# Merge gates and branch projections of a hybrid decoder layer: weights as the moving operand, 1024 columns a unit

## The chip, the cores and the metric

The kernel runs on one core of one Trainium2 chip. The metric is the device time of one execution in microseconds (us). A core has TensorE (matrix multiply; it has a queue for matmuls, PE, and one for loading the stationary operand, PEld), VectorE (DVE), ScalarE (ACT), GpSimd (POOL) and SyncE (SP). In this kernel SP issues nearly all loads and POOL the stores of intermediate results. TensorE writes into PSUM, which the kernel uses as eight banks of 128 partitions x 512 float32: four for the large sums (pool `acc`) and four for small work (pool `mx`).

## What is computed

One decoder layer on 256 tokens with a model width of 4096, in float32. The reference, cut to what matters here (`hgrn2_mix` and `diff_attention` are the two token mixers):

```
u = rmsnorm(h, norm_w[l])                       # [256, 4096]
proj = u @ w_in[l]                              # 10 parts: a_q a_f a_i a_g b_q b_k b_v b_g gate_a gate_b
o_a = hgrn2_mix(a_q, a_f, a_i, lb_all[l])
o_a = rmsnorm(o_a, hgrn_norm_w[l]) * silu(a_g)          # [256, 2048]
o_b = diff_attention(qb, kb, vb, lam, slopes)
o_b = rmsnorm(o_b, subln_w[l]) * (1 - lam_init) * silu(b_g)   # [256, 2048]
y = (sigmoid(gate_a) * (o_a @ w_branch_a[l])    # gate_a, gate_b: [256, 4096]
     + sigmoid(gate_b) * (o_b @ w_branch_b[l]))
h = h + y @ w_out[l]
return rmsnorm(h, final_w)
```

The change touches the projections to `gate_a` and `gate_b` (4096 rows of weights and 4096 columns each) and the two branch projections (2048 rows and 4096 columns each).

## The kernel before

**The stream of weights.** All weights pass through the core once, in pieces of 128 partitions x 2048 float32 (1 MB), 512 pieces in all. SP loads a piece into one of three raw buffers (tile `w`, line 105), up to three pieces ahead. Each piece is split in two halves of 1024 columns. For each half ScalarE writes a rounded part `hi` (line 123) and VectorE the rest, `lo = w - hi` (line 124), both in a format that TensorE takes in one pass. There are four buffers of `hi` and four of `lo`, and the splits run three halves ahead. The activations are split in the same way: `u` (and later `oh` for the outputs of the mixers, `y` for the merged rows) holds for each 128 channels a high and a low part of 256 tokens. A product is then three products: high x hi, high x lo and low x hi.

**Two forms of unit.** In a *stationary* unit (`stat_unit`, `branch_unit`, and `kout_unit` for the forget gates) a 128x128 block of `hi` is loaded into TensorE and the 512 columns of the activations, high and low parts together, move past it (line 184); then the block of `lo` is loaded and the 256 columns of the high part move (line 185). The result has channels as partitions and tokens as columns, in two halves of one bank that must be added (`sum_halves`: ScalarE copies one half, VectorE adds). In a *moving* unit (`mov_unit` with `mov_mm`) 128 tokens of the activations are stationary and 512 columns of weights move, three matmuls for each token block (lines 255 to 257). The result has tokens as partitions.

**The stages.** First come four groups of branch A and four of branch B, with the mixers' small work in between. Then come the merge gates, 64 stationary units of two pieces each; two of them make a tile `gt`, which is scaled, put through a sigmoid and stored to DRAM by POOL (line 286). During this stage the mixers' outputs are reloaded and split into `oh`. Then follow the branch projections, 32 stationary units of two pieces: each loads its gates (tile `gl`, lines 653 and 654), multiplies, adds the two branches and splits the sum into `y`, which has the layout that the output projection wants. The output projection is made of moving units.

**What sets the order.** The program walks through the list of pieces (`run`); for each it issues loads and splits ahead, then the matmuls of both halves, then one step of background work from a list (`todo`). A scheduler then gives each engine its order, which the engine keeps; the splits have a higher priority.

Of the kernel before, what the change touches and what calls it, by code (L numbers as in the profile page):

```python
# [44 lines left out]
def trunk_kernel(ctx, tc, xT, x, nw, w_stat, w_mov, w_a, w_b, w_out, lbt, hnw, lamv, slw, fw, out):  # L45
# [8 lines left out]
    ev = ctx.enter_context(tc.tile_pool(name="ev", bufs=3))  # L54
    gp = ctx.enter_context(tc.tile_pool(name="gp", bufs=2))
# [4 lines left out]
    def f32(ap):  # L60
        return ap.bitcast(F32)

# [124 lines left out]
    def sum_halves(ps, dst=None):  # L187
        t = ev.tile([P, S], F32, name="half", tag="half")
        act.activation(t, ps[:, S:], AF.Copy)
        dst = t if dst is None else dst  # L190
        dve.tensor_tensor(dst, ps[:, :S], t, op=ALU.add)
        return dst
# [82 lines left out]

    def gate_unit(q):
        T = {}

        def gate_done(j):
            def d(ps):  # L280
                if j == 0:
                    T["g"] = gp.tile([P, 2, S], F32, name="gt", tag="gt")
                scaled(ps, T["g"][:, j])
                act.activation(T["g"][:, j], T["g"][:, j], AF.Sigmoid)
                if j == 1:
                    pool.dma_start(g_dram[q], T["g"])
            return d

        for j in range(2):
            stat_unit(48 + q * 2 + j, gate_done(j))  # L290

# [8 lines left out]
    g_dram = [dram.tile([P, 2, S], F32, name=f"g_dram{g}") for g in range(32)]  # L300
# [28 lines left out]
    # ======================= projections and mixers =========================  # L329
    with tc.tile_pool(name="tmp", bufs=1) as tmp:  # L330
# [14 lines left out]
        def finish(T, seg, eps, scale, slot):  # L345
            """rms norm over segments of the channels, times silu of the gate; transposed and out to DRAM."""
# [37 lines left out]
        def rows_done(T, k, then):  # L384
            """Scaled rows out of a unit with the weights moving."""
# [8 lines left out]
        # The 64-token chunks go in pairs. Within a pair the decays count from its middle: exp(b - b_last) and  # L394
        # exp(b_last - b) in the even chunk, exp(b) and exp(-b) in the odd one. From the first pair to the second
        # the keys are decayed to the end of theirs, the queries from the start of theirs.
# [223 lines left out]
        for q in range(4):  # L620
            gate_unit(q)
# [4 lines left out]
    with tc.tile_pool(name="op", bufs=1) as op:  # L626
        oh = [op.tile([P, 4, 2, S], F32R, name=f"oh{g}") for g in range(8)]

        def o_load(g):
            t = op.tile([P, 4, S], F32, name="ol", tag="ol", bufs=2)  # L630
            nc.sync.dma_start(t, o_dram[g])
            return t

        def o_split(g, t):
            act.activation(oh[g][:, :, 0, :], t, AF.Copy)
            dve.tensor_tensor(oh[g][:, :, 1, :], t, f32(oh[g][:, :, 0, :]), op=ALU.subtract)

        ol = {}
        for g in range(8):
            todo.extend([lambda g=g: ol.update({g: o_load(g)}), None, None, lambda g=g: o_split(g, ol.pop(g))])  # L640
        for q in range(4, 32):
            gate_unit(q)

# [1 line left out]
        y = []  # L645

        def branch_unit(m):
            st = {}

            def fn(n, hi, lo):  # L650
                if n == 0:
                    gt = op.tile([P, 2, S], F32, name="gl", tag="gl", bufs=2)
                    nc.sync.dma_start(gt[:, 0], g_dram[m // 2][:, m % 2])
                    nc.sync.dma_start(gt[:, 1], g_dram[16 + m // 2][:, m % 2])
                    st["g"] = gt
                    if m % 4 == 0:
                        y.append(uy.tile([P, 4, 2, S], F32R, name="y", tag="uy"))
                if n % 2 == 0:
                    st["ps"] = acc.tile([P, 512], F32, name="ps_b", tag="acc")
                ps = st["ps"]  # L660
                for k in range(8):
                    kt = 8 * n + k
                    mm_stat(ps, hi[:, k * P : (k + 1) * P], lo[:, k * P : (k + 1) * P], oh[kt // 4], kt % 4,
                            kt % 16 == 0, kt % 16 == 15)
                if n % 2 == 0:
                    return
# [153 lines left out]
```

## Time and profile before

| what | value |
|---|---|
| median of three runs | 2903.52 us (2902.39 to 2905.15) |
| span of the profiled execution (the page gives no other time of it) | 2923.0 us |
| TensorE busy, matmuls | 2909.9 us, 15254 |
| VectorE, ScalarE, GpSimd busy | 1561.8, 1361.9, 97.4 us |
| gate stage, first and last matmul | 1474.63 to 2201.6 us |
| branch stage, first and last matmul | 2201.7 to 2563.4 us |
| output projection, first and last matmul | 2563.5 to 2911.8 us |
| moved by DMA | 583.38 MB, 200 GB/s on average |

In a group of instructions the fields are: line, engine, operation, output tile <- input tiles, shapes, count | busy time in us, mean duration in ns | idle time of the engine just before these instructions, and what ended it. A row of the timeline has start, duration, engine and instruction, and in brackets the idle time before it and what ended it. A row of the stretches has the stretch and its length, then the busy time and count for PE, PEld, DVE, ACT and POOL, the granted clock of TensorE, the busy share of the DMA engines and GB/s. A row of the DMA issues ends with the KB of each and the median us from issue to landing.

### The profile page before, as it was taken

The numbers are of one execution on the slowest core, as the hardware profiler recorded it, in microseconds if no ns is written. First come the engines' busy times: TensorE is split into PE (matmuls) and PEld (weight loads), VectorE is DVE, ScalarE is ACT, GpSimd is POOL, SyncE is SP. The second block draws the span as 40 slices with busy tenths as digits, with TensorE's granted clock in tenths as the row PEclk, the third lists the DMA queues.
The fourth block names the chain that finished last, engine by engine and source line by source line (L and its number), as shares of the span: only waits on it lengthen the run. The fifth ranks groups of instructions, "written<-read, shape, count | busy, mean of one in ns | idle before, by whom it ended". The sixth has DMA issues, their size and how long they took to land.

```text
span 2923.0 us, 37440 instructions
## 1 busy us (share of the span) xinstructions
PE 2909.9 (100%) x15254; PEld 2483.7 (85%) x15254; DVE 1561.8 (53%) x1745; ACT 1361.9 (47%) x1675; POOL 97.4 (3%) x113
## 2 busy tenths in 40 slices
PE   9999999999999999999999999999999999999998
PEld 8888888888888888888888888888888888888886
DVE  6545455464555555555556454545546666654454
ACT  7545454454444444444454444444444444444443
POOL 0000000000000000000000000000000000001010
PEclk9999999999999999999999999999999999999999
DMA  8555555555555555555566555555556556566654
GB/s 333 186 187 187 185 189 180 182 193 187 182 185 185 193 181 190 181 183 194 185 212 241 196 196 200 201 198 198 202 198 207 211 206 211 207 226 210 211 209 173
DMA packets 95277, 583.38 MB, mean 200 GB/s; under 512 B 11376, under 2 KB 19840, under 8 KB 30080
## 3 DMA queue, kind: packets, MB, share of 16 engines
q1 hardware_dynamic: 89568, 562.10, 55.2%
q0 software_dynamic: 5536, 18.89, 1.7%
q8 instruction: 119, 1.95, 0.3%
q14 instruction: 54, 0.44, 0.0%
HBM read 564.17 MB, written 16.78 MB: 199 GB/s over the span
## 4 chain that ended last, share of the span: by engine, by line
PE 95%; issue 3%; DMA 1%; ACT 0%; DVE 0%; POOL 0%; SPq 0%; DVEq 0%; POOLq 0%; ACTq 0%
PE ps_s L184 27%; PE ps_s L185 14%; PE ps_m L255 11%; PE ps_m L256 11%; PE ps_m L257 11%; PE ps_b L184 8%; PE ps_b L185 4%; PE ps_k L184 4%; PE ps_k L185 2%; DMA ol<-o_dram 1%; PE ps_sc L454 0%; PE ps_s L543 0%; PE ps_o L469 0%; DMA o_dram<-oT 0%; PE ps_t L373 0%
## 5 line engine op out<-in xcount | busy, mean ns | idle before, releaser
L124 DVE TENSOR_TENSOR lo<-w,hi 128x1024 fp32r<-128x1024 f32 (+1 forms) x1026 | 1266.7, 1236 | 1292.5 <-ACT hi L123 1291.7
L123 ACT ACTIVATE hi<-w 128x1024 fp32r<-128x1024 f32 (+1 forms) x1026 | 1082.8, 1056 | 1479.4 <-PE ps_s L184 636.9
L184 PE MATMUL ps_s<-u,hi 128*128 128x512 f32 x3584 | 1264.2, 398 | 0.0
L185 PE MATMUL ps_s<-u,lo 128*128 128x256 f32 x3584 | 1007.3, 281 | 0.4 <-DVE lo L124 0.4
L184 PEld LDWEIGHTS ps_s<-u,hi 128*128 128x128 f32 x3584 | 672.9, 188 | 163.5
L185 PEld LDWEIGHTS ps_s<-u,lo 128*128 128x128 f32 x3584 | 677.0, 189 | 1.1 <-DVE lo L124 0.8
L255 PE MATMUL ps_m<-hi,u 128*128 128x512 f32 x1024 | 402.1, 393 | 0.0
L256 PE MATMUL ps_m<-lo,u 128*128 128x512 f32 x1024 | 398.7, 389 | 0.0
L257 PE MATMUL ps_m<-hi,u 128*128 128x512 f32 x1024 | 398.7, 389 | 0.0
L184 PE MATMUL ps_b<-oh,hi 128*128 128x512 f32 x1024 | 361.9, 399 | 0.0
L185 PE MATMUL ps_b<-oh,lo 128*128 128x256 f32 x1024 | 287.6, 281 | 0.0
L184 PEld LDWEIGHTS ps_b<-oh,hi 128*128 128x128 f32 x1024 | 192.4, 188 | 47.9
L257 PEld LDWEIGHTS ps_m<-hi,u 128*128 128x128 f32 x1024 | 192.2, 188 | 40.5
L255 PEld LDWEIGHTS ps_m<-hi,u 128*128 128x128 f32 x1024 | 192.3, 188 | 39.5
L256 PEld LDWEIGHTS ps_m<-lo,u 128*128 128x128 f32 x1024 | 192.3, 188 | 39.0
L255 PE MATMUL ps_m<-hi,y 128*128 128x512 f32 x504 | 196.1, 389 | 0.0
L256 PE MATMUL ps_m<-lo,y 128*128 128x512 f32 x504 | 196.1, 389 | 0.0
L257 PE MATMUL ps_m<-hi,y 128*128 128x512 f32 x504 | 196.1, 389 | 0.0
L185 PEld LDWEIGHTS ps_b<-oh,lo 128*128 128x128 f32 x1024 | 193.4, 189 | 0.0
L184 PE MATMUL ps_k<-u,hi 128*128 128x512 f32 x512 | 180.9, 400 | 0.5 <-DVE u L146 0.4
L185 PE MATMUL ps_k<-u,lo 128*128 128x256 f32 x512 | 141.2, 282 | 0.0
L184 PEld LDWEIGHTS ps_k<-u,hi 128*128 128x128 f32 x512 | 95.8, 188 | 23.9 <-ACT hi L123 1.9
(174 smaller groups left out, 1283.6 us busy)
## 6 DMA issues: line engine op xcount, KB each, us to landing
w<-in_w_stat SPq DMA_DIRECT2D x224, 1024.0 KB, 4.9
w<-in_w_mov SPq DMA_DIRECT2D x156, 1024.0 KB, 4.9
w<-in_w_out SPq DMA_DIRECT2D x64, 1024.0 KB, 4.9
w<-in_w_a SPq DMA_DIRECT2D x32, 1024.0 KB, 5.0
w<-in_w_b SPq DMA_DIRECT2D x32, 1024.0 KB, 4.9
g_dram<-gt POOLq DMA_DIRECT2D x32, 256.0 KB, 3.7
gl<-g_dram SPq DMA_DIRECT2D x64, 128.0 KB, 4.5
o_dram<-oT POOLq DMA_DIRECT2D x8, 512.0 KB, 6.9
```

Of the source, the lines that this page charges most:

```text
L123: act.activation(hi[:, c : c + m], t[:, c : c + m], AF.Copy)
L124: dve.tensor_tensor(lo[:, c : c + m], t[:, c : c + m], f32(hi[:, c : c + m]), op=ALU.subtract)
L184: pe.matmul(ps, wh, ut[:, k].rearrange("p a s -> p (a s)"), start=first, stop=False)
L185: pe.matmul(ps[:, :S], wl, ut[:, k, 0, :], start=False, stop=last)
L255: pe.matmul(ps[t], uh, wh, start=first, stop=False)
L256: pe.matmul(ps[t], uh, wl, start=False, stop=False)
L257: pe.matmul(ps[t], ul, wh, start=False, stop=last)
```

## The change

Gates and branch projections become `wide_unit`s: moving units with 1024 columns of weights. A half piece now holds 128 rows of weights and 1024 columns, as two column halves. For each column half and each of two token blocks there are three matmuls of 512 columns, so that a unit fills all four `acc` banks. The matmuls of a unit's last two half pieces are issued together, bank by bank, and each bank is read out as soon as its six are issued. There are 8 gate units of 16 pieces and 8 branch halves of 8 pieces (for each of four column ranges one of branch A, then one of branch B); the pieces are as many and as large as before.

A gate is now one sigmoid on ScalarE straight from PSUM, which scales by a value for each token, and a store for each 128 x 512 block. At the end of a branch A half VectorE multiplies the four banks by their gates; at the end of a B half it multiplies and adds. As the rows now have tokens as partitions and the output projection needs channels there, each merged 128 x 512 block is turned by four transposes on TensorE (`turn`), a background step, and split into `y` from PSUM. The mixers' outputs are reloaded in 16 blocks of 256 KB in place of 8 of 512 KB, into the four buffers that the gates use too; gates are loaded in four blocks of 256 KB for each branch half.

```diff
-    ev = ctx.enter_context(tc.tile_pool(name="ev", bufs=3))
-    gp = ctx.enter_context(tc.tile_pool(name="gp", bufs=2))
+    gp = ctx.enter_context(tc.tile_pool(name="gp", bufs=4))
...
     def sum_halves(ps, dst=None):
-        t = ev.tile([P, S], F32, name="half", tag="half")
+        t = gp.tile([P, S], F32, name="half", tag="gt")
...
+    def wide_unit(srcs, src_tiles, done):
+        st = {}
+        last = 2 * len(srcs) - 1
+
+        def cols(r, n):
+            c = n if r % 2 else 1 - n
+            return slice(c * 512, (c + 1) * 512)
+
+        def fn(r, hi, lo):
+            if r == 0:
+                st["ps"] = [[acc.tile([P, 512], F32, name="ps_w", tag="acc") for _ in range(2)] for _ in range(2)]
+            ps = st["ps"]
+            if r < last - 1:
+                for n in range(2):
+                    c = cols(r, n)
+                    mov_mm([ps[t][n] for t in range(2)], src_tiles[r // 4], r % 4, hi[:, c], lo[:, c], r == 0, False)
+                return
+            st[r] = hi, lo
+            if r < last:
+                return
+            for n in range(2):
+                for t in range(2):
+                    for k in (last - 1, last):
+                        hi, lo = st[k]
+                        c = cols(k, n)
+                        mov_mm({t: ps[t][n]}, src_tiles[k // 4], k % 4, hi[:, c], lo[:, c], False, k == last, (t,))
+                    done(t, n, ps[t][n])
+
+        add(srcs, fn)
+
     def gate_unit(q):
...
-        for j in range(2):
-            stat_unit(48 + q * 2 + j, gate_done(j))
...
+        def done(t, n, ps):
+            g = gp.tile([P, 512], F32, name="gt", tag="gt")
+            act.activation(g, ps, AF.Sigmoid, scale=rstd[:, t : t + 1])
+            pool.dma_start(g_dram[2 * q + n][t], g)
+
+        wide_unit([w_gate[q, n] for n in range(16)], u, done)
...
-        def branch_unit(m):
...
+        def branch_unit(q):
+            rows, g = {}, {}
+
+            def g_load(br):
+                for n in range(2):
+                    for t in range(2):
+                        gl = g[t, n] = op.tile([P, 512], F32, name="gl", tag="gl", bufs=4)
+                        nc.sync.dma_start(gl, g_dram[8 * br + 2 * q + n][t])
+
+            def a_done(t, n, ps):
+                r = rows[t, n] = gp.tile([P, 512], F32, name="yr", tag="gt")
+                dve.tensor_tensor(r, ps, g[t, n], op=ALU.mult)
+
+            def b_done(t, n, ps):
+                r, gl = rows[t, n], g[t, n]
+                dve.tensor_tensor(gl, ps, gl, op=ALU.mult)
+                dve.tensor_tensor(r, r, gl, op=ALU.add)
+                todo.append(lambda: turn(t, n))
+
+            def turn(t, n):
...
+                ps = mx.tile([P, 4, P], F32, name="ps_y", tag="mx")
+                for j in range(4):
+                    pe.transpose(ps[:, j], rows[t, n][:, j * P : (j + 1) * P], ident)
+                c = slice(t * P, (t + 1) * P)
+                act.activation(yt[:, :, 0, c], ps, AF.Copy)
+                dve.tensor_tensor(yt[:, :, 1, c], ps, f32(yt[:, :, 0, c]), op=ALU.subtract)
+
+            todo.extend([lambda: g_load(0)] + [None] * 7 + [lambda: g_load(1)])
+            wide_unit([w_branch[0, q, n] for n in range(8)], oh[:4], a_done)
+            wide_unit([w_branch[1, q, n] for n in range(8)], oh[4:], b_done)
+
+        for q in range(4):
+            run()
+            branch_unit(q)
...
+def _wide(w):
+    k, n = w.shape
+    w = w.reshape(k // 256, 2, P, n // 1024, 2, 512).transpose(3, 0, 2, 1, 4, 5).reshape(n // 1024, k // 256, P, 4, 512)
+    return w[:, :, :, [1, 0, 2, 3]].reshape(n // 1024, k // 256, P, PIECE)
```

Three places show how the orders of the engines change. The first is TensorE in the branch stage. Before, at the point where one branch unit ends and the next begins (`ps_b` is the bank of the sum, `oh` the activations):

```order
L184 MATMUL ps_b_17248<-oh7_12050,hi_17218 128x512
L185 MATMUL ps_b_17248<-oh7_12050,lo_17219 128x256
L184 MATMUL ps_b_17301<-oh0_12043,hi_17244 128x512
L185 MATMUL ps_b_17301<-oh0_12043,lo_17245 128x256
L184 MATMUL ps_b_17301<-oh0_12043,hi_17244 128x512
L185 MATMUL ps_b_17301<-oh0_12043,lo_17245 128x256
```

And now, where the first B half ends and the next A half begins (`ps_w` are the banks, `yr` a merged block of rows, `ps_y` its turned form; the number behind a name tells one tile from another):

```order
L254 MATMUL ps_w_16177<-hi_16384,oh7_11879 128x512
L255 MATMUL ps_w_16177<-lo_16385,oh7_11879 128x512
L256 MATMUL ps_w_16177<-hi_16384,oh7_11879 128x512
L254 MATMUL ps_w_16177<-hi_16400,oh7_11879 128x512
L255 MATMUL ps_w_16177<-lo_16401,oh7_11879 128x512
L256 MATMUL ps_w_16177<-hi_16400,oh7_11879 128x512
L696 MATMUL ps_y_16449<-ident_99,yr_16142 128x128 x4
L254 MATMUL ps_w_16474<-hi_16462,oh0_11872 128x512
L255 MATMUL ps_w_16474<-lo_16463,oh0_11872 128x512
L256 MATMUL ps_w_16474<-hi_16462,oh0_11872 128x512
```

Pairs of 512 and 256 columns have become triples of 512, and four transposes stand between the units; three more groups of four follow, one after each of the next three pieces.

The second place is ScalarE at the end of a gate unit. Before (`half` is the copied half of a sum, `gt` a gate):

```order
L123 ACTIVATE hi_12716<-w_12666 128x1024
L123 ACTIVATE hi_12737<-w_12666 128x1024
L189 ACTIVATE half_12709<-ps_s_12627 128x256
L123 ACTIVATE hi_12759<-w_12714 128x1024
L284 ACTIVATE gt_12708<-gt_12708 128x256
L123 ACTIVATE hi_12779<-w_12714 128x1024
```

Now, at the end of the second gate unit (`hi_12422` and `hi_12426` are the next unit's first two halves, `hi_12470` and `hi_12490` its third and fourth):

```order
L122 ACTIVATE hi_12422<-w_12386 128x1024
L122 ACTIVATE hi_12426<-w_12386 128x1024
L310 ACTIVATE gt_12436<-ps_w_11898,rstd_118 128x512
L310 ACTIVATE gt_12445<-ps_w_11900,rstd_118 128x512
L310 ACTIVATE gt_12454<-ps_w_11899,rstd_118 128x512
L122 ACTIVATE hi_12470<-w_12420 128x1024
L122 ACTIVATE hi_12490<-w_12420 128x1024
L310 ACTIVATE gt_12463<-ps_w_11901,rstd_118 128x512
```

Four read-outs come together in place of one copy and one sigmoid for each unit, and the fourth stands behind two splits.

The third place is VectorE at the end of a B half (the first one):

```order
L123 TENSOR_TENSOR lo_16463<-w_16456,hi_16462 128x1024
L123 TENSOR_TENSOR lo_16467<-w_16456,hi_16466 128x1024
L686 TENSOR_TENSOR gl_16206<-ps_w_16174,gl_16206 128x512
L686 TENSOR_TENSOR gl_16208<-ps_w_16176,gl_16208 128x512
L687 TENSOR_TENSOR yr_16142<-yr_16142,gl_16206 128x512
L687 TENSOR_TENSOR yr_16150<-yr_16150,gl_16208 128x512
L686 TENSOR_TENSOR gl_16210<-ps_w_16175,gl_16210 128x512
L686 TENSOR_TENSOR gl_16212<-ps_w_16177,gl_16212 128x512
L123 TENSOR_TENSOR lo_16471<-w_16458,hi_16470 128x1024
L123 TENSOR_TENSOR lo_16491<-w_16458,hi_16490 128x1024
L687 TENSOR_TENSOR yr_16158<-yr_16158,gl_16210 128x512
L687 TENSOR_TENSOR yr_16166<-yr_16166,gl_16212 128x512
```

All four products that read PSUM (line 686) stand ahead of the splits of the next unit's second piece; two of the sums (line 687) have moved between them, two behind those splits.

More of the change, by code (lines that the diff above doesn't have):

```diff
@@ L44, in trunk_kernel @@
 @with_exitstack
-def trunk_kernel(ctx, tc, xT, x, nw, w_stat, w_mov, w_a, w_b, w_out, lbt, hnw, lamv, slw, fw, out):
+def trunk_kernel(ctx, tc, xT, x, nw, w_stat, w_mov, w_gate, w_branch, w_out, lbt, hnw, lamv, slw, fw, out):
     nc = tc.nc
@@ L299, in trunk_kernel @@
     o_dram = [dram.tile([P, 4, S], F32, name=f"o_dram{g}") for g in range(8)]
-    g_dram = [dram.tile([P, 2, S], F32, name=f"g_dram{g}") for g in range(32)]
+    g_dram = [[dram.tile([P, 512], F32, name=f"g_dram{b}_{t}") for t in range(2)] for b in range(16)]
     def tables():
@@ L617, in trunk_kernel @@
             run()
-        for q in range(4):
-            gate_unit(q)
+        gate_unit(0)
         run()
@@ L627, in trunk_kernel, with o_load @@
         oh = [op.tile([P, 4, 2, S], F32R, name=f"oh{g}") for g in range(8)]
-        def o_load(g):
-            t = op.tile([P, 4, S], F32, name="ol", tag="ol", bufs=2)
-            nc.sync.dma_start(t, o_dram[g])
-            return t
-        def o_split(g, t):
-            act.activation(oh[g][:, :, 0, :], t, AF.Copy)
-            dve.tensor_tensor(oh[g][:, :, 1, :], t, f32(oh[g][:, :, 0, :]), op=ALU.subtract)
+        def o_load(g, a):
+            t = op.tile([P, 2, S], F32, name="ol", tag="gl", bufs=4)
+            nc.sync.dma_start(t, o_dram[g][:, 2 * a : 2 * a + 2])
+            return t
@@ L638, in trunk_kernel, with o_split @@
+        def o_split(g, a, t):
+            c = slice(2 * a, 2 * a + 2)
+            act.activation(oh[g][:, c, 0, :], t, AF.Copy)
+            dve.tensor_tensor(oh[g][:, c, 1, :], t, f32(oh[g][:, c, 0, :]), op=ALU.subtract)
         ol = {}
         for g in range(8):
-            todo.extend([lambda g=g: ol.update({g: o_load(g)}), None, None, lambda g=g: o_split(g, ol.pop(g))])
-        for q in range(4, 32):
+            for a in range(2):
+                todo.extend([lambda i=(g, a): ol.update({i: o_load(*i)}), None, None, lambda i=(g, a): o_split(*i, ol.pop(i))])
@@ L642, in trunk_kernel @@
+        for q in range(1, 8):
             gate_unit(q)
         y = []
-        def branch_unit(m):
[L648 to L666, printed above, removed]
-                t = sum_halves(ps)
-                dve.tensor_tensor(t, t, st["g"][:, n // 2], op=ALU.mult)
-                if n == 1:
-                    st["t"] = t
-                else:
-                    dve.tensor_tensor(t, t, st["t"], op=ALU.add)
-                    yt = y[m // 4]
-                    act.activation(yt[:, m % 4, 0], t, AF.Copy)
-                    dve.tensor_tensor(yt[:, m % 4, 1], t, f32(yt[:, m % 4, 0]), op=ALU.subtract)
-            add([w_a[m], w_b[m]], fn)
@@ L679, in trunk_kernel @@
-        for m in range(32):
-            branch_unit(m)
+        def branch_unit(q):
[14 more added lines that the diff above has]
+            def turn(t, n):
+                if t == 0:
+                    y.append(uy.tile([P, 4, 2, S], F32R, name="y", tag="uy"))
+                yt = y[2 * q + n]
+                ps = mx.tile([P, 4, P], F32, name="ps_y", tag="mx")
[7 more added lines that the diff above has]
+            wide_unit([w_branch[1, q, n] for n in range(8)], oh[4:], b_done)
@@ L800 @@
         "nw": a["norm_w"][0].reshape(KT, P).T,
-        "w_stat": np.concatenate([_stat(t) for t in (aq, bq, bk, ga, gb)]),
+        "w_stat": np.concatenate([_stat(t) for t in (aq, bq, bk)]),
         "w_mov": np.concatenate([_mov(t) for t in (af, ai, bv, ag, bg)]),
-        "w_a": _stat(a["wa"][0])[:, 0],
-        "w_b": _stat(a["wb"][0])[:, 0],
+        "w_gate": np.concatenate([_wide(ga), _wide(gb)]),
+        "w_branch": np.stack([_wide(a["wa"][0]), _wide(a["wb"][0])]),
         "w_out": _mov(a["wo"][0]),
```

10 lines of the change are left out of this document (removed).

## The prediction

> **What bounds the kernel now.** I read the page first, then the groups of instructions with shapes kept apart, then stretches of the timeline of TensorE in the two forms of matrix work, and last the waits.
>
> ```profile
> span 2923.0 us, 37440 instructions
> PE 2909.9 (100%) x15254; PEld 2483.7 (85%) x15254; DVE 1561.8 (53%) x1745; ACT 1361.9 (47%) x1675; POOL 97.4 (3%) x113
> PEclk9999999999999999999999999999999999999999
> DMA  8555555555555555555566555555556556566654
> L184 PE MATMUL ps_s<-u,hi 128*128 128x512 f32 x3584 | 1264.2, 398 | 0.0
> L185 PE MATMUL ps_s<-u,lo 128*128 128x256 f32 x3584 | 1007.3, 281 | 0.4 <-DVE lo L124 0.4
> L255 PE MATMUL ps_m<-hi,y 128*128 128x512 f32 x504 | 196.1, 389 | 0.0
> ```
>
> TensorE is busy over the whole span at the full clock, and its groups show hardly any idle time ahead of them (the last field). The DMA engines are busy 5 to 6 tenths of the time, VectorE 53%, ScalarE 47%. So TensorE bounds, in each stage that the change touches, and the question is how densely its instructions follow each other. The durations (398, 281, 389 ns) overlap, so a cost has to come from the distance between starts. Three stretches show it: the gate stage (1561 to 2200 us), the branch stage, and the output projection, which already has the form that the change introduces.
>
> ```profile
> 1561.00:2200.00 639.00, 639.00 (x3619) 554.15 (x3618) 319.49 (x339) 272.71 (x340) 15.13 (x28) 1.00 0.57 199
> 2202.00:2562.00 360.00, 360.00 (x2039) 312.32 (x2038) 227.86 (x318) 162.90 (x224) 0.54 (x1) 1.00 0.60 208
> 2564.00:2890.00 326.00, 326.00 (x1440) 269.90 (x1439) 165.43 (x142) 138.05 (x152) 30.75 (x30) 1.00 0.61 213
> ```
>
> The first two stretches hold pairs (a 512-column and a 256-column matmul) for each 128x128 block of weights: 639.0 / (3619/2) = 353.1 ns a pair, 360.0 / (2039/2) = 353.1 ns. The third holds 512-column matmuls alone: 326.0 / 1440 = 226.4 ns each. The start times say the same:
>
> ```profile
> 1699.99 0.40 PE L184 MATMUL ps_s<-u,hi 128*128 128x512 f32 x1
> 1700.23 0.28 PE L185 MATMUL ps_s<-u,lo 128*128 128x256 f32 x1
> ...
> 1711.65 0.40 PE L184 MATMUL ps_s<-u,hi 128*128 128x512 f32 x1
> ...
> 2700.05 0.39 PE L257 MATMUL ps_m<-hi,y 128*128 128x512 f32 x1
> ...
> 2708.89 0.39 PE L257 MATMUL ps_m<-hi,y 128*128 128x512 f32 x1
> ```
>
> 33 pairs take 11.66 us (353.3 ns); 39 matmuls of the moving form take 8.84 us (226.7 ns). I use 353.3 and 226.7.
>
> **The change part by part.** A half piece is 128 partitions x 1024 weights.
>
> *The matrix work, term 1.* A half piece costs 8 pairs = 2.826 us with the weights stationary, and 12 matmuls (two column halves, two token blocks, three products) = 2.720 us with them moving. Both stream 8 x 768 = 12 x 512 = 6144 columns; what differs is 16 instructions against 12. The change moves 64 gate units of four half pieces and 32 branch units of four: 384 half pieces. 384 x 0.106 = **40.7 us less**. The new form's triples are those of the output projection (same line, same shapes, banks changing every three matmuls), so I take its pace; the bounds are that pace and no gain at all.
>
> A rule of the Trainium skill speaks against this term: "TensorE: Matmul & The Clock Gate", section "Back-to-back issue gap", has a matmul of N columns follow the one before after N/2.4 + 2.5 ns. By it, as an estimate, a half piece would go from 2.600 to 2.590 us, and the 384 would gain 4 us in place of 40.7. This trace disagrees with its size: 226.7 ns stand where the rule has 216, and a pair takes 353.3 ns where it has 325.
>
> *The transposes, term 2.* 64 transposes of 128x128 are new on TensorE, in 16 groups of four (the order of TensorE shown with the change). The nearest rows are those that turn the mixers' output:
>
> ```profile
> 776.17 1.04 PE L373 MATMUL ps_t<-ident,o 128*128 128x128 f32 x8
> 776.97 0.48 PE L184 MATMUL ps_s<-u,hi 128*128 128x512 f32 x1
> 777.28 0.28 PE L185 MATMUL ps_s<-u,lo 128*128 128x256 f32 x1
> ```
>
> Eight hold back the next matmul by 0.80 us, and that one's slot is 0.31 us in place of about 0.24: 0.87 us, or 0.109 each: 64 x 0.109 = 7.0. If the longer slot comes with each group, a group of four is 0.40 + 0.08: 16 x 0.48 = 7.7. Bounds: 0, and 16 x (0.48 + 0.16) = 10.2 if a matmul's tail (0.39 less 0.23) shows at each group too. I take **7.3 us more**.
>
> *The boundaries between units, term 3.* A wide unit takes all four accumulator banks, so the next one can start a bank only when it has been read out; before, a unit took one bank of four. With 0 the end of the last matmul's slot, the next unit needs the banks at 0, 0.68, 1.36 and 2.04 us (three matmuls each); their sums are complete (last start + 0.39) at -3.92, -2.56, -1.20 and +0.16, since the last two half pieces are worked off bank by bank, six matmuls each. The prices of the read-outs and of what stands between them:
>
> ```profile
> L389 ACT ACTIVATE v<-ps_m,rstd 128x512 f32<-128x512 f32 x16 | 10.9, 680 | 7.8 <-PE ps_m L257 7.8
> L700 DVE TENSOR_TENSOR hbuf<-ps_m,xr 128x512 f32<-128x512 f32 x16 | 10.3, 682 | 9.1 <-PE ps_m L257 9.1
> L668 DVE TENSOR_TENSOR half<-half,gl 128x256 f32<-128x256 f32 x64 | 27.2, 425 | 2.2
> L123 ACT ACTIVATE hi<-w 128x1024 fp32r<-128x1024 f32 x1018 | 1078.1, 1060 | 1478.3 <-PE ps_s L184 636.9 <-PE ps_m L257 533.4 <-PE ps_b L184 149.2
> L124 DVE TENSOR_TENSOR lo<-w,hi 128x1024 fp32r<-128x1024 f32 x1018 | 1261.4, 1241 | 1291.2 <-ACT hi L123 1290.5
> ...
> 1500.07 1.06 ACT L123 ACTIVATE hi<-w 128x1024 fp32r<-128x1024 f32 x1 [1.77 <-PE ps_s L184]
> 1501.04 0.37 ACT L189 ACTIVATE half<-ps_s 128x256 f32<-128x256 f32 x1
> ...
> 1701.05 0.40 PE L184 MATMUL ps_s<-u,hi 128*128 128x512 f32 x1
> 1701.54 1.06 ACT L123 ACTIVATE hi<-w 128x1024 fp32r<-128x1024 f32 x1 [1.76 <-PE ps_s L184]
> ```
>
> So 0.09 us from a matmul's end to ScalarE (1701.45 to 1701.54), 0.68 for a read-out of 512 columns on either engine, 0.97 from the start of a split to the next instruction of ScalarE. Eight gate units end with four sigmoids, and the order of ScalarE puts the fourth behind both `hi` splits of the next unit's second piece. The first of these waits for the unit's fourth matmul from the end: -0.91 + 0.39 + 0.09 = -0.43, when the third sigmoid also ends (-1.11 + 0.68). The second starts at 0.54, the fourth sigmoid at 1.51; it ends at 2.19, and TensorE goes on at about 2.28 instead of 2.04: 0.24 x 8 = **1.9 us more**. At the four ends of a branch A half VectorE does four products in a row; the last runs from 0.25 to 0.93. At the four ends of B two sums (0.69 each, from 425 ns for half the columns) stand between: the products end at about -2.2, -1.5, 0.5 and 1.2, each ahead of its need. These cost nothing as long as VectorE's cover, the `lo` splits of the next two half pieces, is done by about -2.9, as the buffers freed half a unit's tail earlier (-5.2, then 1.06 and 1.24 us) allow; if one such `lo` came late, its 1.24 us ahead of the fourth product would end it at 2.4 and cost some 0.5 us.
>
> *Held buffers.* The last two half pieces keep their `hi` and `lo` until the end, so the split for the next unit's third half piece starts at -0.43 and its `lo` ends at about 2.4 (behind B's products); TensorE reaches it at 5.4. Cost 0, with 3 us in hand.
>
> *What leaves.* The sums of halves, scalings and small sigmoids were on ScalarE and VectorE, under TensorE's work; their going is worth 0, as they were not on the path.
>
> *Queues.* Gate stores on POOL stay 32 of 256 KB; gate loads on SP become 32 of 256 KB from 64 of 128, the reloads of the mixers' output 16 of 256 KB from 8 of 512. The first four gate loads now stand among unit 1's weights and wait for unit 0's stores.
>
> ```profile
> g_dram<-gt POOLq DMA_DIRECT2D x32, 256.0 KB, 3.7
> gl<-g_dram SPq DMA_DIRECT2D x64, 128.0 KB, 4.5
> w<-in_w_stat SPq DMA_DIRECT2D x224, 1024.0 KB, 4.9
> 1554.55 0.39 PE L185 MATMUL ps_s<-u,lo 128*128 128x256 f32 x1 [0.45 <-DVE lo L124]
> ```
>
> The third store is issued behind its sigmoid at about -0.4 and lands near 4; the weights queued behind its load on SP would have been free to go at 3.2, land at 9 in place of 8, and are split from 13.6. Cost 0. The last row is the only wait of TensorE in the stretch of the reloads; with four smaller buffers I let it stand.
>
> Sum: 2923.0 - 40.7 + 7.3 + 1.9 = **2891.5 us** of span, 31.5 or 1.08% less. The page gives no time of that execution beside its span; the three runs shown have a median of 2903.52, 0.7% under it. I carry the share over: 2903.5 x 0.9892 = **2872 us**.
>
> **The rivals.**
>
> *Pace by columns alone.* If the streamed columns set the pace and a pair's extra time had another cause than its form, term 1 is nil: 2923.0 + 9.2 = 2932.2, scaled 2913. Against it: three stretches with two paces in one execution. Chance 3%. The rule of the Trainium skill cited above ("TensorE: Matmul & The Clock Gate", "Back-to-back issue gap") is close to this case: by it the estimate is 2928, scaled 2909.
>
> *The drains, slower than before.* If at all 16 boundaries the four read-outs queued behind both splits, the first would begin near 0.25 + 2 x 0.97 = 2.2 and TensorE would wait some 3 us: 48 us against a gain of 33.4, so 2937.6, scaled 2918. It decides from 33.4 / 16 = 2.1 us a boundary. Against it: the order has three of four sigmoids, and all products, ahead of those splits. 2%; another 3% for waits near 2.1 us, no difference.
>
> *The drains, in part.* Even if no read-out began before the unit's end, the first would end at 0.93 and the rest keep pace with three matmuls each: about 1 us. 16 x 1 in place of 1.9: 2905.6, scaled 2886. 9%.
>
> *The transposes hide.* Without terms 2 and 3: 2882.3, scaled 2863. 3%.
>
> **How the numbers follow.** The forecast holds the other 80%, with 2866 to 2878 as its own range (term 1 by 2 us, the transposes by 3 and the boundaries by 3, most of them not at once). The range I give, 2861 to 2887, takes in the cheap case and the 1 us boundaries. About 0.2% (5.8 us) is what a measurement of this kernel can tell from no change: faster 80 + 9 + 3 = 92, same 3, slower 3 + 2 = 5.
>
> **What would show it.** Gate and branch stretches with 226 to 227 ns between matmul starts; 16 groups of four `ps_y` transposes, each holding TensorE back about 0.45 us; at a gate unit's end one TensorE wait of 0.2 to 0.3 us on a `gt` sigmoid, and none on the products. The forecast is wrong if the new triples run slower than those of the output projection, if waits of 1 us or more stand at the units' starts, or if TensorE waits for `lo` in the third or fourth half piece of a unit.

## The result, and the profile after

| | time, median (lowest to highest) | span of its profiled execution |
|---|---|---|
| before, beside the change | 2914.22 us (2902.39 to 2923.48), 10 executions | 2922.96 us |
| after | 2894.44 us (2893.32 to 2895.92), 10 executions | 2892.47 us, its own time 2894.51 |

The ratio is 0.9936, with a 95% interval of 0.9912 to 0.9959: the change makes the kernel faster, by 0.6%; its slowest execution is 6.5 us below the fastest of before. I had forecast 2872 us and a range of 2861 to 2887, and the time lies outside it. Yet the span that my sum gave, 2891.5 us, is within 1.0 us of the measured one. The forecast of the work was close against that execution, and what I did to it in its last line was wrong.

The table holds the key. The times of before are wide apart, and not spread evenly: five lie between 2902.4 and 2905.8 us, five between 2922.6 and 2923.5, none between. Over all comparisons of this study 50 executions of before lie at 2901 to 2906 us, and 45 at 2920 to 2925. The lower group starts at 2901 to 2902 us in each comparison, so I compare kernels across them. The three times that stand ahead of the prediction are all of the lower group; the profiled execution, with a span of 2923.0, was of the upper. In every execution that has both, the time is 1.7 to 2.1 us above the span.

The page of the kernel after, and its groups of TensorE (duration and count):

```profile
span 2892.5 us, 33800 instructions
PE 2878.5 (100%) x13782; PEld 2412.5 (83%) x13782; DVE 1478.8 (51%) x1497; ACT 1326.0 (46%) x1507; POOL 97.4 (3%) x113
L254 PE MATMUL ps_w<-hi,u 128*128 128x512 f32 x1024 | 399.6, 390 | 0.0
L255 PE MATMUL ps_w<-lo,u 128*128 128x512 f32 x1024 | 399.0, 390 | 0.8 <-DVE lo L123 0.8
L254 PE MATMUL ps_w<-hi,oh 128*128 128x512 f32 x512 | 200.6, 392 | 0.0
L696 PE MATMUL ps_y<-ident,yr 128*128 128x128 f32 x64 | 9.6, 271 | 0.0
```

TensorE still bounds, with the same instructions as in the output projection. In the two changed stages its matmuls show one wait, of 0.8 us; the queue of weight loads shows more, which come further down. In the timeline of the gate stage 33 matmuls of the new form, first and last:

```profile
1644.10 0.39 PE L254 MATMUL ps_w<-hi,u 128*128 128x512 f32 x1
...
1651.58 0.39 PE L254 MATMUL ps_w<-hi,u 128*128 128x512 f32 x1
```

7.48 us / 33 = 226.7 ns each, the pace that I took. The stretches between the stages' first matmuls, worked out from the start times of each trace, in us (the output stage runs to the end of the last matmul):

| | up to the gates | gates | branches | output | rest | span |
|---|---|---|---|---|---|---|
| before (upper group) | 1474.6 | 727.1 | 361.8 | 348.7 | 10.8 | 2923.0 |
| before, profiled again (lower group) | 1474.3 | 714.2 | 355.0 | 348.6 | 10.8 | 2902.9 |
| after | 1473.6 | 703.1 | 354.8 | 350.2 | 10.8 | 2892.5 |

Against the upper group the gates take 24.0 us less, and the branches with the output 5.5 less. Against the lower group the gates take 11.0 less, and the branches with the output 1.4 more. So the experiments have to tell what the two groups of before are, and whether the terms of the sum are what I said.

### The profile page after: what moved, and what is told of

Same layout as the page of the kernel before. It is cut to its first block, busy times and chain, and to the rows that moved or that the text cites. A ratio compares the mean times of both kernels' runs of the same rounds, so it can differ in the third digit from the quotient of the medians.

```text
span 2892.5 us, 33800 instructions
## 1 busy us (share of the span) xinstructions
PE 2878.5 (100%) x13782; PEld 2412.5 (83%) x13782; DVE 1478.8 (51%) x1497; ACT 1326.0 (46%) x1507; POOL 97.4 (3%) x113
## 3 DMA queue, kind: packets, MB, share of 16 engines
q8 instruction: 108, 1.77, 0.2%
## 4 chain that ended last, share of the span: by engine, by line
PE 95%; issue 3%; DMA 1%; ACT 0%; DVE 0%; SPq 0%; POOL 0%; DVEq 0%; ACTq 0%; POOLq 0%
PE ps_s L183 12%; PE ps_m L254 12%; PE ps_m L255 12%; PE ps_m L256 12%; PE ps_w L254 11%; PE ps_w L255 11%; PE ps_w L256 11%; PE ps_s L184 6%; PE ps_k L183 4%; PE ps_k L184 2%; DMA ol<-o_dram 1%; PE ps_sc L477 0%; PE ps_s L566 0%; PE ps_o L492 0%; PE ps_y L696 0%
## 5 line engine op out<-in xcount | busy, mean ns | idle before, releaser
L183 PE MATMUL ps_s<-u,hi 128*128 128x512 f32 x1536 | 540.2, 396 | 0.0
L184 PE MATMUL ps_s<-u,lo 128*128 128x256 f32 x1536 | 431.7, 281 | 0.0
L255 PE MATMUL ps_w<-lo,u 128*128 128x512 f32 x1024 | 399.0, 390 | 0.8 <-DVE lo L123 0.8
L254 PE MATMUL ps_w<-hi,u 128*128 128x512 f32 x1024 | 399.6, 390 | 0.0
L256 PE MATMUL ps_w<-hi,u 128*128 128x512 f32 x1024 | 398.4, 389 | 0.0
L183 PEld LDWEIGHTS ps_s<-u,hi 128*128 128x128 f32 x1536 | 288.0, 188 | 67.8 <-DVE half L190 0.2
L184 PEld LDWEIGHTS ps_s<-u,lo 128*128 128x128 f32 x1536 | 290.1, 189 | 0.3
L254 PEld LDWEIGHTS ps_w<-hi,u 128*128 128x128 f32 x1024 | 192.2, 188 | 42.7 <-ACT gt L310 2.6
L255 PEld LDWEIGHTS ps_w<-lo,u 128*128 128x128 f32 x1024 | 192.2, 188 | 40.7 <-DVE lo L123 1.1
L256 PEld LDWEIGHTS ps_w<-hi,u 128*128 128x128 f32 x1024 | 192.2, 188 | 39.9
L254 PE MATMUL ps_w<-hi,oh 128*128 128x512 f32 x512 | 200.6, 392 | 0.0
L256 PE MATMUL ps_w<-hi,oh 128*128 128x512 f32 x512 | 199.4, 389 | 0.0
L255 PE MATMUL ps_w<-lo,oh 128*128 128x512 f32 x512 | 199.3, 389 | 0.0
L254 PE MATMUL ps_m<-hi,y 128*128 128x512 f32 x504 | 196.5, 390 | 0.0
```

Source lines behind the costliest of these rows:

```text
L183: pe.matmul(ps, wh, ut[:, k].rearrange("p a s -> p (a s)"), start=first, stop=False)
L184: pe.matmul(ps[:, :S], wl, ut[:, k, 0, :], start=False, stop=last)
L254: pe.matmul(ps[t], uh, wh, start=first, stop=False)
L255: pe.matmul(ps[t], uh, wl, start=False, stop=False)
L256: pe.matmul(ps[t], ul, wh, start=False, stop=last)
```

## The experiments

**Before once more.** The same kernel, profiled again and timed, to see whether its two groups differ in the work or around it.

> The kernel before, unchanged, looked at again. Its ten times lie in two groups, 2902 to 2906 and 2922 to 2924 us, and the profile shown is of the second. Two paces: a stationary pair (512 and 256 columns) runs at 346.7 or at 353.3 ns, and which of the two lasts until something disturbs TensorE; an execution near 2904 then has the gate and branch stages (3072 pairs) at 346.7, 20 us less than at 353.3, and all else as before. Rival, time outside TensorE: both groups have pairs at 353 ns, and the 19 us lie in waits, transfers or around the span.

Seven executions took 2901.2 to 2904.6 us, three 2922.4 to 2923.8. The profile fell in the lower group this time. Its stretches of the gate and the branch stage:

```profile
1561.00:2200.00 639.00, 639.00 (x3689) 563.44 (x3688) 326.09 (x347) 277.58 (x346) 15.67 (x29) 1.00 0.58 203
2202.00:2540.00 338.00, 338.00 (x1952) 298.03 (x1951) 218.94 (x307) 155.64 (x214) 0.00 (x0) 1.00 0.62 213
```

TensorE is just as busy and its clock is full, but 3689 matmuls fit where the first profile had 3619: 639.0 / (3689/2) = 346.4 ns a pair in place of 353.1. The difference lies inside the span, in the distance between matmuls. And the first profile shows the place where it begins, around the wait that my prediction quoted and "let stand". The timeline of TensorE in the profile of before:

```profile
1514.54 0.39 PE L184 MATMUL ps_s<-u,hi 128*128 128x512 f32 x1
...
1553.71 0.39 PE L184 MATMUL ps_s<-u,hi 128*128 128x512 f32 x1
1554.55 0.39 PE L185 MATMUL ps_s<-u,lo 128*128 128x256 f32 x1 [0.45 <-DVE lo L124]
1554.77 0.39 PE L184 MATMUL ps_s<-u,hi 128*128 128x512 f32 x1
1555.00 0.28 PE L185 MATMUL ps_s<-u,lo 128*128 128x256 f32 x1
1555.12 0.40 PE L184 MATMUL ps_s<-u,hi 128*128 128x512 f32 x1
...
1556.89 0.40 PE L184 MATMUL ps_s<-u,hi 128*128 128x512 f32 x1
```

Ahead of the wait 113 pairs take 39.17 us, 346.6 ns each. Behind it five pairs take 1.77 us, 354 ns, and the pace of 353.3 then holds to the end of the branch stage, through 1008 us. That is some 1008 / 0.3533, about 2850 pairs; at 6.67 ns each the slower pace costs 19.0 us, beside the 0.7 us of the wait. The two spans differ by 20.1. In the lower group's profile that wait isn't there. What differs ahead of it is when the last reload of a mixer's output lands and is split. ScalarE and VectorE in the first profile of before:

```profile
1551.04 1.06 ACT L635 ACTIVATE oh<-ol 128x1024 fp32r<-128x1024 f32 x1 [2.89 <-DMA ol<-o_dram]
1552.13 1.23 DVE L636 TENSOR_TENSOR oh<-ol,oh 128x1024 fp32r<-128x1024 f32 x1 [2.16 <-ACT oh L635]
1553.28 1.22 DVE L124 TENSOR_TENSOR lo<-w,hi 128x1024 fp32r<-128x1024 f32 x1
```

and in the second:

```profile
1549.32 1.06 ACT L635 ACTIVATE oh<-ol 128x1024 fp32r<-128x1024 f32 x1 [2.44 <-DMA ol<-o_dram]
1550.41 1.23 DVE L636 TENSOR_TENSOR oh<-ol,oh 128x1024 fp32r<-128x1024 f32 x1 [1.72 <-ACT oh L635]
1551.55 1.22 DVE L124 TENSOR_TENSOR lo<-w,hi 128x1024 fp32r<-128x1024 f32 x1
```

The order of VectorE is the same. With the reload landed and its split 1.7 us later, the `lo` behind it comes too late for TensorE. Why the reload lands later in some executions stays open. From here on I call 346.7 ns the fast pace and 353.3 the slow one.

**The reload's splits tied to pieces.** If the wait picks the slow pace, a kernel without the wait should have one group only. Before, with the `oh` splits made to depend on the current half piece, so that they cannot cluster:

```diff
+            dve.tensor_scalar(pace[:, g : g + 1], f32(run.hi[:, 0:1]), 0.0, 1.0, op0=ALU.mult, op1=ALU.add)
-            act.activation(oh[g][:, :, 0, :], t, AF.Copy)
+            act.activation(oh[g][:, :, 0, :], t, AF.Copy, scale=pace[:, g : g + 1])
```

> The kernel before, with the eight splits of the reloaded mixer outputs tied to eight pieces of the gate stage, 20 us apart (a scale of exactly 1.0 that depends on a piece), in place of a burst within 35 us. Two paces: the wait of TensorE at 1554 us, behind which the pace of the profiled execution changes from 347 to 353 ns, is gone, and the pace set by the transposes at 1511 us (347 ns) stays to the end of the branch stage: 2902 to 2905 us in all executions, one group. If the other pace is what stays, all lie near 2922. Rival, the groups have nothing to do with that wait: times in both groups as before.

2902.02 us (2900.78 to 2902.58), all twelve executions in one group, while of the 35 of before beside them 18 lay at 2901.4 to 2904.0 and 17 at 2920.9 to 2924.7. The trace has no wait in the stretch of the reloads, gates of 714.2 and branches of 355.0 us. The upper group is gone with the wait. I did not add a wait to a kernel without one, so that the wait acts by itself rests on the trace above and on a second one, of the branches alone, below; that a disturbance of TensorE can do it is shown further down.

**The gates alone, the branches alone.** Each kernel has one of the two stages in the new form and the other as before. Between the stages the gates are not brought into the layout that the next one reads; bytes and instructions are the same.

```diff
-        for j in range(2):
-            stat_unit(48 + q * 2 + j, gate_done(j))
+        wide_unit([w_gate[q, n] for n in range(16)], u, done)
```

> Only the gates become wide units; the branch projections stay stationary and their gates are loaded from blocks of the wrong layout, so the output is not the reference's (same bytes, same instructions). Two paces: the gate stage takes 256 x 2.720 = 696 us and some 4 us of waits; the branch stage 1024 pairs at 346.7 (355.0 us) or 353.3 (361.8). Against the changed kernel (2894.4) that is 7.3 us less for the transposes, 348.2 less and 355.0 or 361.8 more: 2894 or 2901 us. Rival, one pace of 353.3 for pairs and a fixed share around the span as the prediction had it: 0.9933 x (2923 - 27.1 + 1.9) = 2879 us.

2897.53 us (2896.37 to 2899.13, twelve executions), one group. The forecast for slow branches was 2901; the profiled execution took 2899.1, and the output stage, without the transposes, 1.6 us less than after. In the trace the gates take 703.0 us, as in the full change, and the branches, still pairs, 361.8. They start right behind triples and run at the slow pace throughout, as the branch stage's stretch shows:

```profile
2202.00:2540.00 338.00, 338.00 (x1913) 292.91 (x1912) 214.22 (x299) 152.51 (x210) 0.00 (x0) 1.00 0.59 208
```

```diff
-            add([w_a[m], w_b[m]], fn)
+            wide_unit([w_branch[0, q, n] for n in range(8)], oh[:4], a_done)
+            wide_unit([w_branch[1, q, n] for n in range(8)], oh[4:], b_done)
```

> Only the branch projections become wide units, with their transposes; the gates stay stationary units and are loaded with the wrong layout, so the output is not the reference's (same bytes, same instructions). Two paces: the gate stage has 2048 pairs at 346.7 (710 us) or 353.3 (723.6 us) in place of 700 us in the changed kernel (2894.4): 2904 or 2918 us, possibly both in different executions. So the branch part alone gains nothing on the faster group of the kernel before. Rival, one pace of pairs: 0.9933 x (2923 - 13.6 + 7.3) = 2897 us.

Nine executions took 2903.0 to 2904.2 us, three 2916.2 to 2916.9; the profile fell among the three, with gates of 726.8 us and branches of 355.0. So the gates, still pairs, carry their two groups with them, 12.8 us apart. In this trace, too, the pace changes at a late `lo` while the reload is being split:

```profile
1538.94 1.23 DVE L123 TENSOR_TENSOR lo<-w,hi 128x1024 fp32r<-128x1024 f32 x1
1540.06 0.39 PE L183 MATMUL ps_s<-u,hi 128*128 128x512 f32 x1
1540.22 0.19 PEld L184 LDWEIGHTS ps_s<-u,lo 128*128 128x128 f32 x1
```

The `lo` ends at 1540.17 us, and the weight load that needs it starts at 1540.22, 0.16 us after the matmul ahead of it and not together with it, as elsewhere. The pair takes 390 ns. Ahead of it 86 pairs stand at 346.7 ns; behind it 31 at 353.2, and after a wait of 0.20 us at 1551.66 the same pace holds to the end of the stage. So here some 43 ns of delay mark the change of pace.

The new branch stage by itself gains nothing over before's lower group (355.0 with the fast pace, and here 355.0 plus 1.6 us of transposes in the output stage): what 12 matmuls in place of 16 save is given back by the transposes. Against slow pairs it gains 361.8 - 355.0 = 6.8.

**TensorE alone.** To see whether the pace needs DMA or other engines at all, a small kernel, run once, has the same forms of matmul with nothing beside them: stretches of pairs, with some transposes, plain float32 matmuls or triples ahead of each, and at the end four times 64 matmuls of one size.

```diff
+    for n in (1, 2, 3, 4, 1, 2, 3, 4):
+        turns(n)
+        pairs(48)
+    for cols in (512, 384, 256, 128):
+        equal(64, cols)
```

> Nothing of the layer is computed (the output is zero): TensorE alone, fed from one tile, runs moving triples of 512 columns, stationary pairs of 512 and 256, single sizes of 512, 384, 256 and 128 columns, and between stretches of 48 pairs one to four transposes or plain float32 matmuls as a disturbance. Two paces: triples start every 226.7 ns; pairs stand at 346.7 or 353.3 ns a pair, constant within a stretch, and which one follows the disturbance, with no DMA and no other engine at work. A fixed price for each matmul would show as N/2.4 + 13.3 ns: 226.7, 173.3, 120 and 66.7 ns. Rival, the slower pace comes from ScalarE, VectorE or DMA traffic: all stretches at 346.7.

Both paces appear, at the full clock, with VectorE and ScalarE idle and the DMA engines at most 1% busy. The timeline shows 46 pairs that follow two transposes, first and last, and 46 that follow four:

```profile
182.86 0.38 PE L61 MATMUL ps_turn<-ident,w 128*128 128x128 f32 x2
183.00 0.47 PE L41 MATMUL ps_pair<-u,hi 128*128 128x512 f32 x1
183.31 0.28 PE L42 MATMUL ps_pair<-u,lo 128*128 128x256 f32 x1
183.43 0.40 PE L41 MATMUL ps_pair<-u,hi 128*128 128x512 f32 x1
...
199.38 0.40 PE L41 MATMUL ps_pair<-u,hi 128*128 128x512 f32 x1
...
217.50 0.39 PE L41 MATMUL ps_pair<-u,hi 128*128 128x512 f32 x1
...
233.75 0.40 PE L41 MATMUL ps_pair<-u,hi 128*128 128x512 f32 x1
```

15.95 us / 46 = 346.7 ns against 16.25 / 46 = 353.3. The start times of all stretches:

```
ahead of the pairs          pace of the pairs
triples (64, 4, 5)          slow, slow, slow
1 transpose (twice)         fast, fast
2 transposes                fast
3 transposes (twice)        slow, fast
4 transposes (twice)        slow, slow
plain float32 1, 2, 1, 3    fast, fast, fast, slow
one form, distance of starts: 512 columns 226.8 ns, 384: 173.7, 256: 119.8, 128: 110.9
```

(The scheduler put the first case's transpose and one of the second's at the program's start; the table has what TensorE ran.) So TensorE's own instructions are enough to pick the pace, at the last disturbance, and it persists. Their number alone does not decide: three transposes were followed by the slow pace once and by the fast one once. The last line explains the fast pace. From 256 to 512 columns a matmul with its own weight load takes N / 2.4 + 13.3 ns: 226.7, 173.3, 120.0. A pair at that price is 226.7 + 120.0 = 346.7 ns, and the slow pace is this plus 6.67 ns, the time of 16 columns at that slope. What inside TensorE costs it stays open.

The rule of the Trainium skill that the prediction weighed ("TensorE: Matmul & The Clock Gate", "Back-to-back issue gap") has N / 2.4 + 2.5 ns for isolated matmuls at the full clock. The slope agrees with these distances; the constant is 13.3 here.

**A chosen pace.** If that is so, the pace of the real branch stage can be chosen. The kernel with the tied reload gets one dummy transpose just ahead of the first branch matmul, or, with `range(4)`, four.

```diff
+                if m == 0 and n == 0:
+                    pk = mx.tile([P, 4, P], F32, name="ps_kick", tag="mx")
+                    for j in range(1):
+                        pe.transpose(pk[:, j], ident, ident)
```

> The kernel before with the reload's split spread over the pieces, and one dummy 128x128 transpose on TensorE just ahead of the first matmul of the branch stage; nothing else. Without the dummy that kernel had its branch stage at 355.0 us (pairs at 346.7 ns) and took 2902.0. Theory: a disturbance of TensorE itself picks the pace of the pairs that follow, and one transpose left them at 346.7 ns in the run on TensorE alone: branch stage 355.0 us, time about 2902. Rival (the pace isn't picked by what stands on TensorE just ahead): the same 2902, so this run only tells something beside the one with four.

> As the run with one dummy transpose, but with four at the same place. Theory: four transposes left the pairs that followed at 353.3 ns both times in the run on TensorE alone, so the 1024 pairs of the branch stage take 1024 x 6.67 = 6.8 us more: branch stage 361.8 us, time about 2909. Rival (the pace is picked by something else than TensorE's own sequence, such as a transfer or a wait): only the three more transposes are paid, some 0.3 us, branch stage 355.3 us, time about 2902.4.

With one: 2902.11 us (2901.00 to 2903.36). With four: 2909.27 us (2908.21 to 2910.06), ten executions each, the groups apart. The branch stage's stretch with one, then with four:

```profile
2202.00:2540.00 338.00, 338.00 (x1952) 298.02 (x1951) 218.90 (x305) 155.13 (x214) 0.00 (x0) 1.00 0.62 213
```

```profile
2202.00:2540.00 338.00, 338.00 (x1915) 293.12 (x1914) 214.25 (x298) 152.08 (x210) 0.00 (x0) 1.00 0.60 210
```

The counts, 1952 and 1915, are those that this stretch has in the two profiles of before, lower and upper group. Three more transposes, 0.3 us of work, cost 7.2 us. The rival (2902.4) falls.

**Without the transposes.** After, with the merged rows split as they stand; the 64 transposes are left out.

```diff
-                ps = mx.tile([P, 4, P], F32, name="ps_y", tag="mx")
-                for j in range(4):
-                    pe.transpose(ps[:, j], rows[t, n][:, j * P : (j + 1) * P], ident)
+                ps = rows[t, n].rearrange("p (a c) -> p a c", a=4)
```

> The changed kernel without its 64 transposes on TensorE: the merged rows are split into y as they stand, from SBUF, so the output is not the reference's. If a transpose costs what the prediction took (0.109 to 0.12 us each, nothing hidden), the branch stage and the total are 7.0 to 7.7 us shorter than the changed kernel: 2887 us. Rival, the transposes run where TensorE would wait anyway: 2894 us.

2884.76 us (2884.22 to 2886.17), 9.7 below after. In the traces the branches take 348.8 us in place of 354.8 and the output 348.6 in place of 350.2: 7.6 us for 16 groups, 0.48 each. Ahead of the branches, where the two kernels are alike, the traces differ by another 0.8. The remaining 1.3 us is no part of the traces: this profiled execution was the slowest of its five (2886.17). The first group of transposes in the trace of after:

```profile
2263.84 0.39 PE L256 MATMUL ps_w<-hi,oh 128*128 128x512 f32 x1
2264.07 0.60 PE L696 MATMUL ps_y<-ident,yr 128*128 128x128 f32 x4
2264.42 0.48 PE L254 MATMUL ps_w<-hi,oh 128*128 128x512 f32 x1
2264.74 0.40 PE L255 MATMUL ps_w<-lo,oh 128*128 128x512 f32 x1
```

0.35 us for four, and 0.32 in place of 0.23 for the slot behind them: the 0.09 comes with each group. That is 0.44 us a group, and 7.1 over all 16 by the starts; the other 0.5 of the 7.6 I have not traced.

**The sigmoids ahead of the splits.** After, with the gates' read-outs at a higher priority than the `hi` splits:

```diff
-            act.activation(g, ps, AF.Sigmoid, scale=rstd[:, t : t + 1])
+            with tc.high_priority(4 * AHEAD):
+                act.activation(g, ps, AF.Sigmoid, scale=rstd[:, t : t + 1])
```

> The changed kernel with the sigmoids that read out a gate unit's banks given a higher priority than the splits, so that the fourth stands behind one split and not behind two. The eight waits of TensorE on a gate sigmoid (3.0 us in the trace of the changed kernel) go: 2891.4 us. Rival, the waits are given back by later splits: 2894 us.

2889.99 us (2888.45 to 2891.90). The gates take 701.1 us in place of 703.1 and the branches, at whose head the eighth boundary stands, 354.5 in place of 354.8. None of the eight waits on a sigmoid is left, and the reload's waits are some 0.3 us shorter. In after each of them looks like this, in the queue of weight loads and in that of the matmuls:

```profile
1567.81 0.19 PEld L254 LDWEIGHTS ps_w<-hi,u 128*128 128x128 f32 x1 [0.38 <-ACT gt L310]
```

```profile
1567.46 0.39 PE L256 MATMUL ps_w<-hi,u 128*128 128x512 f32 x1
1567.81 0.50 PE L254 MATMUL ps_w<-hi,u 128*128 128x512 f32 x1
1568.14 0.40 PE L255 MATMUL ps_w<-lo,u 128*128 128x512 f32 x1
```

The weight load stands for 0.38 us, but it runs ahead of its matmul: the two slots take 0.35 + 0.33 in place of 2 x 0.227, so a boundary costs 0.23 us and the eight of them 1.8. The other 3.5 us by which the spans differ lie in the stages before the gates, whose pairs the edit does not touch. Their distances account for it: 1983 of these pairs stand 350.4 ns apart on average in this trace and 352.2 in that of after, 3.5 us in all. So the paces of the early pairs change from run to run.

**The two edits together.** After, with the sigmoids first and the reload tied to pieces.

> The changed kernel with sigmoids first and with the 16 reloads of the mixers' outputs tied to 16 pieces, 20 us apart, as in the spread kernel. Gate waits of 3.0 us and the wait of about 1 us on a lo in the reload go: 2890.4 us, in one group. Against the spread kernel (2902.0) that is what moving weights are worth when pairs already run at 346.7: 3072 x 6.67 ns = 20.5 less 7.3 for the transposes = 13 us, so 2889. Rival, a part of the gain needs the slower pairs: 2894 or more.

2887.86 us (2885.87 to 2889.04), ratio 0.9929 (0.9901 to 0.9956). Gates of 700.1 us; no wait of TensorE is left in them. It beats both kernels.

**And a transpose at the start of stretches.** The same, with one dummy transpose at twelve places of the early stages where pairs begin.

```diff
+    def kick():
+        pk = mx.tile([P, 4, P], F32, name="ps_kick", tag="mx")
+        pe.transpose(pk[:, 0], ident, ident)
```

> The change with the sigmoids' higher priority and the spread reload (2887.9 us), and one dummy transpose at the twelve places where a stretch of pairs begins in the early stage. Theory: a single transpose sets the pairs that follow to 346.7 ns; some 660 of the early pairs ran at 353.3 ns in that kernel's profile, 660 x 6.67 = 4.4 us, less 12 transposes with the pair behind them at about 0.1 us each, 1.2: 3.2 us less, about 2884.7. Rival: the small matmuls of the mixers, which stand between pieces, set the pace anew behind each dummy: no gain, 1.2 us more, 2888 to 2889.

2885.41 us (2884.76 to 2886.41), the lowest of the complete kernels, and below the run before it by 2.4 us, on another chip. The trace bears out only part of the reason. Three stretches of 127 pairs, each right behind a dummy, run at 346.7 ns where they had 353.3, 2.5 us less. But 136 pairs from 49 to 98 us went the other way, 0.9 us more; the dummy nearest to them ran at 35.8 us, with pairs in another order between. And three stretches of 79 pairs stay at 353.3 behind small matmuls of the mixers that run after the dummy, as the rival had it. The mean distance of the early pairs fell from 348.9 to 348.1 ns, 1.7 us, and the twelve dummies take about 1.2 of it by the estimate in the expectation. The spans of the two profiled executions differ by 0.6 us only, so most of the 2.4 us is not explained by these traces.

In each place where a stretch of pairs stands right behind a single transpose, it ran at the fast pace: seven times here, twice in the run on TensorE alone, once in the kernel with one dummy. Behind groups of eight both paces occur (in the kernel with the tied reload, 159 pairs at 353.3 ns from 774.8 us, and 159 at 346.7 from 959.3). What decides there I can't say.

## Why the prediction was right, and where it failed

*What bounds the kernel*: right. TensorE is without a gap before and after, at the full clock, and every gain is in the number of its instructions and their distance.

*The matrix work (term 1)*: right against the execution that I read, and half of it only against the other kind. I took 353.3 ns for a pair from three views, and they agreed because they all lay behind the same wait. In that execution the gates went from 727.1 to 703.1 us, 24.0 less. I had 256 x 0.106 less 1.9 = 25.2; some 124 pairs from 1511 us to the wait, which ran at the fast pace already, make 0.8 of the difference, and 0.5 is a longer wait for the reload. With fast pairs a half piece is 8 x 346.7 = 2.773 us against 2.720, and term 1 is 384 x 0.053 = 20.5 us, not 40.7. Of the 40.7, 20.5 are four instructions fewer for each half piece at 13.3 ns (384 x 4 x 13.3), which the change always brings, and 20.5 are slow pairs (384 x 8 x 6.67), which it brings only where there were any.

*The transposes (term 2)*: right. 7.6 us by the run without them, 7.1 by the starts of the matmuls, for a forecast of 7.3. The longer slot comes with each group, as the 7.7 had it, but four transposes hold the next matmul back by 0.35 us and not by 0.40.

*The boundaries (term 3)*: right in place, mechanism and size. One wait at each gate unit's end, on the fourth sigmoid, and none at the branches. 0.23 us each by the starts of the matmuls (0.24 forecast), 1.8 us in all (1.9 forecast). The run with the sigmoids first is 2.3 us shorter in the two stages, 0.3 of it in the reload's waits.

*Held buffers, queues, what leaves*: right at 0. Gate stores land in 5.9 us in place of 3.7, and TensorE does not wait for them.

*The reload's wait, let stand*: nearly right in after, where it grew from 0.7 to 1.2 us by the starts of the matmuls, but in before this was the row that decided. I took 0.45 us for its price. It cost some 20.

*The last line, "I carry the share over"*: **the step that failed.** The span of 2923.0 was 19.5 us above the median of the times. I took this for something like the cost of profiling, scaled the forecast by 2903.5 / 2923.0, and so took 19.5 us off a forecast that needed nothing taken off. The runs show that an execution's time is 1.7 to 2.1 us above its span, so the profiled execution was a slower one than the three beside it. Two sums would have come close: 2891.5 plus 2 us, 2893.5, since after has no slow pairs in the stages that matter; or the lower group's 2903.5 - 20.5 + 7.3 + 1.9 = 2892.2, to which the longer wait adds 0.5. Measured: 2894.4. Both need the question that I did not ask: where in the trace are the 20 us by which this execution is longer than its fellows? That the 2891.5 us came within 1.0 of the span is in part luck: the changed stages and the output took 29.5 us less, not 31.5, and the stages ahead of the gates, which the change does not touch, happened to be 1.0 shorter.

*The rivals*: none of them was this one. "Pace by columns alone" asked whether a pair's extra time came from its form. Half of it depends on how TensorE was last disturbed, but I weighed only all or nothing, and dismissed it by three stretches of one execution.

*The chances*: faster held.

## What to carry to other kernels

When the profiled execution's span does not fit the times beside it, find the difference in the trace before using either: here a span of 20 us above the times meant another kind of execution, and a factor put over the whole forecast was the largest error of all. Compare the pace of the same instructions ahead of and behind each wait, not only the length of the wait; a 0.45 us wait that changes the pace of 2850 pairs costs 20 us. And where the same work can be done with fewer, longer matmuls of one size, as here, it gains the fixed 13.3 ns of each one left out; the triples showed one pace only, 226.7 ns.

## What the runs showed of the hardware that I had not expected

- Alternating 512- and 256-column matmuls with their own weight loads run at 346.7 or 353.3 ns a pair, with the clock at 1.00 in both. The pace is picked at the last disturbance of TensorE (a wait, transposes, another form) and stays, here for over 1000 us; in one trace it changes at a pair delayed by 43 ns. Four transposes ahead of a stretch gave the slow pace in the run on TensorE alone and in the kernel, triples gave it in all four places where pairs stood right behind them, and one transpose gave the fast pace wherever pairs followed it at once; three and eight gave both.
- In this format a matmul's slot is N / 2.4 + 13.3 ns at 256, 384 and 512 columns (119.8, 173.7, 226.8 ns); at 128 columns it is 110.9 ns, not 66.7.
- The first matmul behind a group of one to eight 128x128 transposes takes some 0.08 to 0.09 us more.
- A weight load that stands for 0.38 us costs its matmul 0.23: read the cost of such a wait from the starts of the matmuls.
